# Two levels of a gated unit's decay tree in one TensorE step, on copies made by ScalarE

## The chip, the cores and the metric

The kernel runs on one core of a Trainium2 chip. The metric is device time in microseconds (us) of one execution, as the median of several runs. TensorE (PE) does the matrix products, VectorE (DVE) and ScalarE (ACT) the elementwise work, GpSimd (POOL) clears tiles, SyncE (SP) issues nearly all transfers.

## The reference

One decoder layer over 2048 tokens of width 1024, in f32. Its first half mixes tokens with three kinds of heads in parallel; the second half is a gated MLP of width 2816 with a causal convolution of width 3. The change is in the first half, in the heads that compute

```
S_t = diag(exp(log_f_t)) S_{t-1} + k_t^T v_t,   o_t = q_t S_t
```

for HGRN2 heads (forget gate from a sigmoid) and GLA heads (low-rank gate). Here the decay differs for each key channel and token, so within a chunk the scores are

```
attn[i, j] = sum_d q[i, d] k[j, d] exp(cum[i, d] - cum[j, d]),   j <= i
```

which is no plain product of q and k. The third kind, retention, has one decay for a head and needs no such care. Each head's output is normalised, gated, and the heads together go through one output projection.

## The kernel before

**Blocks and units.** The mixer works through four blocks of 512 tokens (`NB`, `TB`). In each block seven units follow each other in `ORDER`: h0, g, h1, h2, h3, r0, r1. An h unit is two HGRN2 heads (`unit_h`), g is four GLA heads in two halves (`unit_g`), r is two retention heads (`unit_r`). A unit begins with its input projections: long rows of f32 products, each split in three passes (`split3`, lines 290 to 292) of a high and a low part. They are TensorE's main stream. What is left of a unit is small work in many dependent steps, which is laid between the products of later units. After the last unit of a block come the output projection (`out_half`, `out_finish`) and the next block's norm. After block 3 follows the MLP, in products that the change does not touch.

**A gated unit (`gated`).** Scores inside 128 tokens are built by a tree. `LEVELS` are 1, 2, 4, 8, 16, 32, 64. At level s, queries in the odd runs of s tokens meet keys in the even run just ahead. Between two levels, q of the odd runs and k of the even runs are multiplied in place by the decay of a run (`tree[li]`, lines 743 and 745, on DVE), so that at each level a plain product gives the right scores. A level step is thus: 16 to 32 small products in tiles of 32 columns into a bank `lev` (line 737), then on DVE the two multiplications in place, which must wait until TensorE has read the old values, and then the scores go to their places: by a masked copy into `near` (line 749, up to level 16) or by ACT into the score tile `at` (line 756). At level 16 ACT also copies `near` into `at` (line 760). Ahead of the levels, products "dots" (`dt`) give the diagonal, which line 722 lays into `near`. Behind the levels k is transposed (`kT`), then come the products u with the update of the state (`carry`), the outputs o (`attn_out`), their norm and gate (`post`), and, some time later, their transpose (`transposed`) for the output projection.

**The order.** TensorE's order is written out by hand, that of the other engines is partly planned by priorities (`tc.high_priority`). A planner's clock (`Clock`) counts the nominal time of the products emitted so far (`adv`). A step that must wait for other engines is not emitted at once; its generator yields a gap, and the next step is emitted into the stream when that time has passed. `chain` lets one gated unit or retention unit at a time go through its steps; at `yield None` the next may begin. A tuple as a gap is a ride (`ride`): from its first time on the step goes right behind the next level step (`clock.pick`), at its second time at the latest alone. `until` runs due steps ahead of their time if something must be done by then. The constants of the gaps stand in lines 50 to 55:

```
LEVEL_GAP = (3.2, 4.2)
POST_GAP = 14.0
LAND = 6.0
FIRST_GAP = 1.8, 0.8
RIDE = (1.8, 6.0), (3.4, 7.6)
STAT_GAP, NORM_GAP = 2.4, 1.6
```

`LEVEL_GAP` lies between levels (h units, g units), `FIRST_GAP` behind the dots and after level 1, `RIDE` ahead of u and o, `POST_GAP` ahead of the transpose of an output. `STAT_GAP` and `NORM_GAP` space the parts of the norms, `LAND` is the time that a sum of weights waits for its loads.

**Side work.** DVE also computes sums for the MLP's block products (`weight_sums`, `early_sums`) and products of the conditioning vector (`ada`). These are tied behind a DVE instruction that was noted last (`marked`, `pinned`), so that they aren't put ahead of it.

Of the kernel before, what the change touches and what calls it, by code (L numbers as in the profile page):

```python
# [122 lines left out]
def trunk(ctx, tc, xT, vecs, cvec, cst, rope, msk, wada, win, walow, wgla, wout, wup, wdown, out):  # L123
# [125 lines left out]
    def marked(op):  # L249

        mark[:] = [op.ins]
# [317 lines left out]
    def norm1_stat(b):  # L569
        acc = new_acc(f"n1_{b}")  # L570

        def part(k):
            x = tmp(f"x{b}_{k}")
            nc.sync.dma_start(x[:], xT[b, :, k, :])
            sumsq(acc, x, k, f"n1_{b}_")
        for k in range(KD):
            clock.at(STAT_GAP * k, lambda k=k: part(k))
        bc1[b] = new_bc1(b)
        clock.ride(rstd(acc, f"n1_{b}", bc1[b][:], lambda: done.add(("n1", b)), gap=14.0), 24.0, 28.0)

# [27 lines left out]
    def tok_evac(vsg, pss):  # L608
        v, sg = vsg
        for j, ps in enumerate(pss):  # L610
            p3 = ps[:].rearrange("p (c n) -> p c n", n=256)
            c2 = slice(2 * j, 2 * j + 2)
            S.copy(v[:, c2, :], p3[:, :, 0:P])
            S.activation(sg[:, c2, :], p3[:, :, P:256], AF.Sigmoid)
            V.tensor_tensor(sg[:, c2, :], sg[:, c2, :], p3[:, :, P:256], op=ALU.mult)

    def tok_evac4(vsg, pss, at):

        v, sg = vsg
        for c, ps in enumerate(pss):  # L620
            gate = ps[:, at + P:at + 256]
            S.copy(v[:, c, :], ps[:, at:at + P])
            S.activation(sg[:, c, :], gate, AF.Sigmoid)
            V.tensor_tensor(sg[:, c, :], sg[:, c, :], gate, op=ALU.mult)

    def post(o, sg, name):
# [9 lines left out]
        V.tensor_tensor(o8, o8, rs[:].unsqueeze(2).to_broadcast([P, 8, 64]), op=ALU.mult)  # L636
        V.tensor_tensor(o[:], o[:], sg[:], op=ALU.mult)

# [27 lines left out]
    def carry(b, Sst, ps, decay):  # L666

        W = wide.pop(0)
        wide.append(W)
        at = pu.tile([P, NCH - 1, 64], F32, tag="Sc", name="Sc", bufs=3)  # L670
        halves = slice(0, 64), slice(64, P)
# [28 lines left out]
    def gated(name, b, ui, pos, kq, q, decay, subs, qk, sel):  # L700
# [14 lines left out]
        nh = 2 * len(subs)  # L715
        ps = late_ps("dt" + name)
        for c in range(NCH):
            tiled(ps[:, c * nh:(c + 1) * nh], qk[:, c * P:(c + 1) * P], sel)
        pairs = ps[:, 0:NCH * nh].rearrange("p (a n) -> p a n", n=len(subs))
        with tc.high_priority(offset=CHAIN):  # L720
            for i, near in enumerate(nears):
                V.copy_predicated(near[:], m_all[:, 80:112].unsqueeze(1).to_broadcast([P, 8, 32]),
                                  pairs[:, :, i:i + 1].to_broadcast([P, 8, 32]))
        adv(ML)
        yield FIRST_GAP[0]
        for li, s in enumerate(LEVELS):
            w = max(32, 2 * s)
            cols = slice(0, 128 if s < 64 else 256)
            pss = [lev_ps(f"lv{name}_{s}") for _ in parts]
            for c in range(NCH):  # L730
                for k0 in [g for g in range(0, P, 32) if g % w < max(s, 32)]:
# [3 lines left out]
                    for ps, rs in zip(pss, parts):  # L735
                        rhs = q[rs, :, at:at + w].rearrange("p h (n t s) -> p h n t s", t=2, s=s)[:, :, :, 1, :]
                        T.matmul(ps[p0:p0 + 32, n * w:(n + 1) * w].rearrange("p (h n s) -> p h n s", h=2, s=s),
                                 kq[rs, c * P + k0:c * P + k0 + 32], rhs, start=True, stop=True)
            with tc.high_priority(offset=CHAIN):
                ev = tree[li]  # L740
                nn = TB // (2 * s)
                qv = q[:].rearrange("p h (n t s) -> p h n t s", t=2, s=s)[:, :, :, 1, :]
                V.tensor_tensor(qv, qv, ev[:, :, 0:1].unsqueeze(1).to_broadcast([P, 2, nn, s]), op=ALU.mult)
                kv = kq[:].rearrange("p (n t s) -> p n t s", t=2, s=s)[:, :, 0, :]
                marked(V.tensor_tensor(kv, kv, ev[:, :, 1:2].to_broadcast([P, nn, s]), op=ALU.mult))
                for ps, at, near in zip(pss, attns, nears):
                    if s <= 16:
                        mk = m_all[:, 16 * li:16 * li + 16].rearrange("p (n s) -> p n s", s=s)
                        V.copy_predicated(near[:].rearrange("p a (n t s) -> p a n t s", t=2, s=s)[:, :, :, 1, :],
                                          mk.unsqueeze(1).to_broadcast([P, 8, 16 // s, s]),  # L750
                                          ps[:, cols].rearrange("p (a n s) -> p a n s", a=8, s=s))
                    else:
                        for r0 in range(0, P, w):
                            for odd in range(2):
                                p0 = r0 + s * odd
                                S.copy(at[r0:r0 + s, :].rearrange("p (c o h n) -> p c o h n", c=2, o=2, h=2)[:, :, odd, :, r0 + s:r0 + w],
                                       ps[p0:p0 + s, cols].rearrange("p (c h n) -> p c h n", c=2, h=2))
                    if s == 16:
                        for r0 in range(0, P, 32):
                            S.copy(at[r0:r0 + 32, :].rearrange("p (a n) -> p a n", a=8)[:, :, r0:r0 + 32],  # L760
                                   near[r0:r0 + 32])
            adv(ML)
            clock.pick()
            if s < LEVELS[-1]:
                yield LEVEL_GAP[two] + (FIRST_GAP[1] if s == 1 else 0.0)
        yield None
        yield LEVEL_GAP[two]
        ps = late_ps("kT" + name)
# [38 lines left out]
    def unit_h(b, u, pos):  # L807
# [38 lines left out]
    def unit_g(b, pos):  # L846
# [32 lines left out]
        for i in range(2):  # L879
# [3 lines left out]
            subs.append((rows, *tok_tiles(f"{nm}_{i}")))  # L883
        clock.chain(gated(nm, b, 4, pos, kq, q, decay, subs, qk, selg), 14.0)
        pss = tf512(f"vg{nm}", 18)
# [5 lines left out]
    def unit_r(b, r, pos):  # L891
# [16 lines left out]
        for x, y in zip(a, bb):  # L908
# [136 lines left out]
    def out_half(b, half, acc=None, after_pieces=None, begun=(), own=None):  # L1045
        all_done()
        for i in range(4):
# [3 lines left out]
            for m in (2 * i, 2 * i + 1):  # L1051
# [696 lines left out]
```

## Time and profile before

| what | value |
|---|---|
| median of 3 runs | 2422.54 us (2421.09 to 2425.87) |
| the profiled execution's own time | 2418.1 us |
| its span, first to last instruction | 2416.3 us |
| busy of TensorE | 2382.3 us, 99% |
| busy of VectorE | 1811.7 us, 75% |
| busy of ScalarE | 1229.3 us, 51% |
| busy of GpSimd | 154.2 us, 6% |
| mean granted TensorE clock | 0.998 |

The span is shorter than the execution's own time by what lies around the instructions. Busy time is the union of an engine's instructions; TensorE's overlap in its pipeline, so that the mean length of one is longer than the distance from one start to the next. In the groups of instructions, a row gives line, engine, operation, output and inputs by the program's names, shapes and count, then busy time, mean ns of one, and the engine's idle time just ahead of them with what ended it.

### The profile page before, as it was taken

The numbers are of one execution on the slowest core, as the hardware profiler recorded it, in microseconds if no ns is written. First come the engines' busy times: TensorE is split into PE (matmuls) and PEld (weight loads), VectorE is DVE, ScalarE is ACT, GpSimd is POOL, SyncE is SP. The second block draws the span as 40 slices with busy tenths as digits, with TensorE's granted clock in tenths as the row PEclk, the third lists the DMA queues.
The fourth block names the chain that finished last, engine by engine and source line by source line (L and its number), as shares of the span: only waits on it lengthen the run. The fifth ranks groups of instructions, "written<-read, shape, count | busy, mean of one in ns | idle before, by whom it ended". The sixth has DMA issues, their size and how long they took to land.

```text
span 2416.3 us, 51796 instructions
## 1 busy us (share of the span) xinstructions
PE 2382.3 (99%) x20523; PEld 1962.8 (81%) x20523; DVE 1811.7 (75%) x3391; ACT 1229.3 (51%) x2191; POOL 154.2 (6%) x275
## 2 busy tenths in 40 slices
PE   7999999999999999999999999999999999999998
PEld 5788878878788878888788888888878888888887
DVE  7687766877577746767988888966878787778666
ACT  4565445644565446535645554554545454555442
POOL 1000000000000000001000000000010110000000
PEclk9999999999999999999999999999999999999999
DMA  7665676896788758778554444686765444447663
GB/s 273 228 214 186 226 271 224 293 329 237 258 311 290 259 187 284 267 260 295 178 170 155 148 155 144 229 281 218 226 204 173 144 149 139 153 151 271 210 196 118
DMA packets 228883, 525.78 MB, mean 218 GB/s; under 512 B 25848, under 2 KB 28832, under 8 KB 228640
## 3 DMA queue, kind: packets, MB, share of 16 engines
q1 hardware_dynamic: 225440, 511.98, 63.1%
q0 software_dynamic: 3200, 10.49, 1.2%
q8 instruction: 161, 2.64, 0.4%
q14 instruction: 82, 0.67, 0.1%
HBM read 392.87 MB, written 129.50 MB: 216 GB/s over the span
## 4 chain that ended last, share of the span: by engine, by line
PE 84%; DVE 6%; DMA 5%; issue 3%; ACT 1%; SPq 0%; POOL 0%; DVEq 0%; ACTq 0%; POOLq 0%
PE X L290 6%; PE X L291 6%; PE X L292 6%; PE Z L291 3%; PE Z L292 3%; PE Z L290 3%; PE dX L290 3%; PE dX L292 3%; PE dX L291 3%; PE psqkvgr L290 3%; PE psqkvgr L291 2%; PE psqkvgr L292 2%; PE psvgh L290 2%; PE y L290 2%; PE y L291 2%
## 5 line engine op out<-in xcount | busy, mean ns | idle before, releaser
L290 PE MATMUL X<-B,A 128*128 128x512 f32 x572 | 223.1, 390 | 0.5 <-ACT u L1424 0.3
L291 PE MATMUL X<-B,A 128*128 128x512 f32 x572 | 222.8, 389 | 0.3 <-DVE B L1121 0.2
L292 PE MATMUL X<-B,A 128*128 128x512 f32 x572 | 222.6, 389 | 0.0
L1121 DVE TENSOR_TENSOR dA<-rd,dA 128x512 fp32r<-128x512 f32 x154 | 106.1, 690 | 89.8 <-ACT dA L1120 89.6
L1120 ACT CAST dA<-rd 128x512 fp32r<-128x512 f32 x154 | 95.6, 621 | 143.7 <-PE dX L292 58.0
L290 PE MATMUL dX<-dB,dA 128*128 128x512 f32 x396 | 154.1, 389 | 1.3 <-DVE y L1606 1.3
L292 PE MATMUL dX<-dB,dA 128*128 128x512 f32 x396 | 154.0, 389 | 0.0
L291 PE MATMUL dX<-dB,dA 128*128 128x512 f32 x396 | 154.0, 389 | 0.0
L1121 DVE TENSOR_TENSOR A<-s,A 128x512 fp32r<-128x512 f32 x176 | 120.6, 686 | 39.5 <-ACT A L1120 39.4
L290 PE MATMUL psvgh<-hvgh,ha 128*128 128x256 f32 x480 | 140.3, 292 | 0.0
L1120 ACT CAST A<-s 128x512 fp32r<-128x512 f32 x176 | 108.5, 617 | 56.9 <-PE Z L292 41.9
L291 PE MATMUL psvgh<-lvgh,ha 128*128 128x256 f32 x480 | 135.6, 283 | 0.0
L292 PE MATMUL psvgh<-hvgh,ha 128*128 128x256 f32 x480 | 135.6, 282 | 0.0
L290 PEld LDWEIGHTS X<-B,A 128*128 128x128 f32 x572 | 107.3, 188 | 24.0 <-ACT u L1424 1.1
L291 PEld LDWEIGHTS X<-B,A 128*128 128x128 f32 x572 | 107.4, 188 | 23.0 <-DVE B L1121 1.0
L292 PEld LDWEIGHTS X<-B,A 128*128 128x128 f32 x572 | 107.4, 188 | 22.3
L291 PE MATMUL Z<-B,A 128*128 128x512 f32 x308 | 120.5, 391 | 1.4 <-DVE B L1121 1.2
L290 PE MATMUL Z<-B,A 128*128 128x512 f32 x308 | 120.3, 391 | 0.1
L292 PE MATMUL Z<-B,A 128*128 128x512 f32 x308 | 119.9, 389 | 0.0
L1120 ACT CAST A<-r 128x512 fp32r<-128x512 f32 x132 | 82.3, 623 | 63.8 <-PE Z L292 58.5
L1121 DVE TENSOR_TENSOR A<-r,A 128x512 fp32r<-128x512 f32 x132 | 90.6, 687 | 31.8 <-ACT A L1120 31.6
L1121 DVE TENSOR_TENSOR dB<-rb,dB 128x512 fp32r<-128x512 f32 x154 | 105.6, 687 | 9.9 <-ACT dB L1120 9.5
(480 smaller groups left out, 6714.3 us busy)
## 6 DMA issues: line engine op xcount, KB each, us to landing
gs<-yv SPq DMA_DIRECT2D x154, 256.0 KB, 3.0
rb<-gs SPq DMA_DIRECT2D x154, 256.0 KB, 4.2
r<-wup SPq DMA_DIRECT2D x143, 256.0 KB, 3.5
s<-sumsu SPq DMA_DIRECT2D x132, 256.0 KB, 3.0
wada<-wada SPq DMA_DIRECT2D x48, 512.0 KB, 4.9
rd<-sumsd SPq DMA_DIRECT2D x88, 256.0 KB, 3.9
rd<-wdown SPq DMA_DIRECT2D x66, 256.0 KB, 3.8
x<-xT SPq DMA_DIRECT2D x64, 256.0 KB, 5.9
```

What stands on the lines that cost most here:

```text
L290: T.matmul(ps, lhs[0], rhs[0], start=first, stop=False, skip_group_check=more)
L291: T.matmul(ps, lhs[0], rhs[1], start=False, stop=False, skip_group_check=more)
L292: T.matmul(ps, lhs[1], rhs[0], start=False, stop=last, skip_group_check=more)
L1120: S.copy(hi, src)
L1121: V.tensor_tensor(lo, src, hi, op=ALU.subtract)
```

## The change

- The levels go in pairs (1, 2), (4, 8), (16, 32); 64 stays alone. For a pair, ACT copies the odd runs of q and all of k to new tiles `qc` and `kc_` (`ahead`); then DVE scales q and k in place for the second level (`faded`). TensorE then does the first level from the copies and the second from q and k, in one step into one bank. After it DVE scales q and k for the next level, ACT copies again, both levels are laid into their places (`laid`), and DVE scales once more.
- The dots go into the first pair's step.
- The gaps: between pairs 5.2 us (h) and 6.4 us (g), 7.6 us ahead of the first pair, 4.0 us ahead of `kT`; `yield None` comes behind the pair (16, 32) instead of behind level 64. Chains start 1.5 us earlier after their call.
- Outputs are transposed 21 us after their step, rides of state updates get later windows, loads and norms get more time; a sum of squares is emitted 3 us after its load.
- More DVE instructions are `marked`: gates, the end of `post`, and the residual sums of the output projection.
- The tile `Sc` has 2 buffers instead of 3.
- Retention units of block 2 start after 14.5 instead of 11 us.

```diff
-POST_GAP = 14.0
-LAND = 6.0
-FIRST_GAP = 1.8, 0.8
-RIDE = (1.8, 6.0), (3.4, 7.6)
-STAT_GAP, NORM_GAP = 2.4, 1.6
+POST_GAP = 21.0
+LAND = 7.5
+FIRST_GAP = 7.6
+PAIR_GAP = (5.2, 6.4)
+RIDE = (2.4, 7.4), (3.8, 9.0)
+STAT_GAP, STAT_LAND, NORM_GAP = 2.4, 3.0, 2.0
...
-            sumsq(acc, x, k, f"n1_{b}_")
+            clock.at(STAT_LAND, lambda: sumsq(acc, x, k, f"n1_{b}_"))
...
-        clock.ride(rstd(...), 24.0, 28.0)
+        clock.ride(rstd(...), 26.0, 30.0)
...
+    qc = p1.tile([P, 2, TB // 2], F32, tag="qc", name="qc")
+    kc_ = p1.tile([P, TB], F32, tag="kc", name="kc")
...
-            V.tensor_tensor(sg[:, c2, :], sg[:, c2, :], p3[:, :, P:256], op=ALU.mult)
+            marked(V.tensor_tensor(sg[:, c2, :], sg[:, c2, :], p3[:, :, P:256], op=ALU.mult))
...
+        def faded(li):
+            s, ev = LEVELS[li], tree[li]
+            nn = TB // (2 * s)
+            qv = q[:].rearrange("p h (n t s) -> p h n t s", t=2, s=s)[:, :, :, 1, :]
+            V.tensor_tensor(qv, qv, ev[:, :, 0:1].unsqueeze(1).to_broadcast([P, 2, nn, s]), op=ALU.mult)
+            kv = kq[:].rearrange("p (n t s) -> p n t s", t=2, s=s)[:, :, 0, :]
+            marked(V.tensor_tensor(kv, kv, ev[:, :, 1:2].to_broadcast([P, nn, s]), op=ALU.mult))
+        def ahead(li):
+            s = LEVELS[li]
+            S.copy(qc[:].rearrange("p h (n s) -> p h n s", s=s),
+                   q[:].rearrange("p h (n t s) -> p h n t s", t=2, s=s)[:, :, :, 1, :])
+            S.copy(kc_[:], kq[:])
+        def level(li, first):
...
+                        T.matmul(ps[p0:p0 + 32, o + n * w:o + (n + 1) * w].rearrange("p (h n s) -> p h n s", h=2, s=s),
+                                 (kc_ if first else kq)[rs, c * P + k0:c * P + k0 + 32], rhs, start=True, stop=True)
+        def laid(li, first):
...
+        with tc.high_priority(offset=CHAIN):
+            ahead(0)
+            faded(0)
+        yield FIRST_GAP
+        for li in range(0, 8, 2):
+            pss = [lev_ps(f"lv{name}_{li}") for _ in parts]
+            pair_ = li < 6
+            if li == 0:
+                dots = late_ps("dt" + name)
+                for c in range(NCH):
+                    tiled(dots[:, c * nh:(c + 1) * nh], qk[:, c * P:(c + 1) * P], sel)
+            if pair_:
+                level(li, True)
+                level(li + 1, False)
+            else:
+                level(li, False)
+            with tc.high_priority(offset=CHAIN):
+                faded(li + 1 if pair_ else li)
+                if li < 4:
+                    ahead(li + 2)
+                if li == 0:
+...
+                laid(li, pair_)
+                if pair_:
+                    laid(li + 1, False)
+                if li < 4:
+                    faded(li + 2)
+            adv((2 if pair_ else 1) * ML)
+            clock.pick()
+            if li == 4:
+                yield None
+            if pair_:
+                yield PAIR_GAP[two]
+        yield 4.0
...
-        clock.chain(gated(nm, b, u, pos, kq, q, decay, subs, qk, selh), 9.0 if b == u == 0 else 6.0)
+        clock.chain(gated(nm, b, u, pos, kq, q, decay, subs, qk, selh), 7.5 if b == u == 0 else 4.5)
...
-        clock.chain(retention(nm, b, r, pos, a[0], kk, kc, q, vsg), 14.5 if b < 2 else 11.0)
+        clock.chain(retention(nm, b, r, pos, a[0], kk, kc, q, vsg), 14.5 if b < 3 else 11.0)
...
-                    V.scalar_tensor_tensor(x1[m], ps[:], G1[:, m:m + 1], x1[m], op0=ALU.mult, op1=ALU.add)
+                    marked(V.scalar_tensor_tensor(x1[m], ps[:], G1[:, m:m + 1], x1[m], op0=ALU.mult, op1=ALU.add))
```

More of the change, by code (lines that the diff above doesn't have):

```diff
@@ L578, in norm1_stat @@
         bc1[b] = new_bc1(b)
-        clock.ride(rstd(acc, f"n1_{b}", bc1[b][:], lambda: done.add(("n1", b)), gap=14.0), 24.0, 28.0)
+        clock.ride(rstd(acc, f"n1_{b}", bc1[b][:], lambda: done.add(("n1", b)), gap=14.0), 26.0, 30.0)
     def norm1_h(b):
@@ L715, in gated @@
         nh = 2 * len(subs)
[L716 to L726, printed above, removed]
+        def faded(li):
[11 more added lines that the diff above has]
+        def level(li, first):
+            s = LEVELS[li]
             w = max(32, 2 * s)
-            cols = slice(0, 128 if s < 64 else 256)
-            pss = [lev_ps(f"lv{name}_{s}") for _ in parts]
+            o = 0 if first else 128
             for c in range(NCH):
@@ new lines, in laid @@
+        def laid(li, first):
+            s = LEVELS[li]
+            w = max(32, 2 * s)
+            o = 0 if first else 128
+            cols = slice(o, o + (128 if s < 64 else 256))
+            for ps, at, near in zip(pss, attns, nears):
+                if s <= 16:
+                    mk = m_all[:, 16 * li:16 * li + 16].rearrange("p (n s) -> p n s", s=s)
+                    V.copy_predicated(near[:].rearrange("p a (n t s) -> p a n t s", t=2, s=s)[:, :, :, 1, :],
+                                      mk.unsqueeze(1).to_broadcast([P, 8, 16 // s, s]),
+                                      ps[:, cols].rearrange("p (a n s) -> p a n s", a=8, s=s))
+                else:
+                    for r0 in range(0, P, w):
+                        for odd in range(2):
+                            p0 = r0 + s * odd
+                            S.copy(at[r0:r0 + s, :].rearrange("p (c o h n) -> p c o h n", c=2, o=2, h=2)[:, :, odd, :, r0 + s:r0 + w],
+                                   ps[p0:p0 + s, cols].rearrange("p (c h n) -> p c h n", c=2, h=2))
+                if s == 16:
+                    for r0 in range(0, P, 32):
+                        S.copy(at[r0:r0 + 32, :].rearrange("p (a n) -> p a n", a=8)[:, :, r0:r0 + 32],
+                               near[r0:r0 + 32])
@@ new lines, in gated @@
+        with tc.high_priority(offset=CHAIN):
[12 more added lines that the diff above has]
+                level(li + 1, False)
+            else:
+                level(li, False)
+            with tc.high_priority(offset=CHAIN):
+                faded(li + 1 if pair_ else li)
+                if li < 4:
+                    ahead(li + 2)
+                if li == 0:
+                    pairs = dots[:, 0:NCH * nh].rearrange("p (a n) -> p a n", n=len(subs))
+                    for i, near in enumerate(nears):
+                        V.copy_predicated(near[:], m_all[:, 80:112].unsqueeze(1).to_broadcast([P, 8, 32]),
+                                          pairs[:, :, i:i + 1].to_broadcast([P, 8, 32]))
+                laid(li, pair_)
[4 more added lines that the diff above has]
+            adv((2 if pair_ else 1) * ML)
+            clock.pick()
+            if li == 4:
+                yield None
+            if pair_:
+                yield PAIR_GAP[two]
```

41 lines of the change are left out of this document (7 added, 34 removed).

## The prediction

> **What bounds the kernel now.** I read the page first, then busy time by stage, then TensorE's own waits, then single steps in the timeline.
>
> ```profile
> span 2416.3 us, 51796 instructions
> ...
> PE 2382.3 (99%) x20523; PEld 1962.8 (81%) x20523; DVE 1811.7 (75%) x3391; ACT 1229.3 (51%) x2191; POOL 154.2 (6%) x275
> ```
>
> TensorE is busy in 99% of the span; nothing else is near. So the time falls only if TensorE gets less to do or waits less. The mixer, where the change lies, runs from about 60 to 1110 us. The next view is busy time by stretch (columns: stretch, length, busy of PE, PEld, DVE, ACT, POOL, then clock and DMA; the last row sums four stretches).
>
> ```profile
> 330.00:620.00 290.00, 286.84 (x3817) 233.88 (x3816) 206.93 (x521) 145.64 (x300) 13.61 (x24) 1.00 0.77 266
> ...
> sum 1050.00, PE 1043.46 PEld 859.14 DVE 748.33 ACT 545.60 POOL 52.24; mean PE 260.87 PEld 214.78 DVE 187.08 ACT 136.40 POOL 13.06
> ```
>
> The granted clock is 1.00 here, and TensorE idles 1050.00 - 1043.46 = 6.5 us. That is all that better timing of steps could give. Its longest wait there, in the list of waits:
>
> ```profile
> PE lvh L737 <- DVE orsh L180: 1.5, 1, 1.5
> ```
>
> If there is more to win it is hidden in "busy": what a small block costs TensorE when it cuts into the stream of large products. One level step of an h unit, with its neighbours (columns: start, length, engine, line, what):
>
> ```profile
> 308.80 0.39 PE L291 MATMUL y<-oTh,hwo 128*128 128x512 f32 x1
> 309.03 0.39 PE L292 MATMUL y<-oTh,lwo 128*128 128x512 f32 x1
> 309.35 0.46 PE L737 MATMUL lvh<-qbh,kh 128*32 128x32 f32 x32
> 309.74 0.51 PE L290 MATMUL y<-oTr,hwo 128*128 128x512 f32 x1
> 310.08 0.40 PE L291 MATMUL y<-oTr,hwo 128*128 128x512 f32 x1
> ...
> 313.36 0.46 PE L737 MATMUL lvh<-qbh,kh 128*32 128x32 f32 x32
> ```
>
> Large products follow each other every 0.23 us (308.80 to 309.03). From 309.03 to 310.08 there are 1.05 us for two of them, 0.46 us, and the step: the step takes 0.59 us. Of this 0.09 lies ahead of the level (309.35 against 309.26), and 0.11 in the first large product behind it, which lasts 0.34 to the next start. The same for a unit g, whose step has twice as many:
>
> ```profile
> 114.71 0.28 PE L291 MATMUL psvgh<-lvgh,ha 128*128 128x256 f32 x1
> 114.83 0.28 PE L292 MATMUL psvgh<-hvgh,ha 128*128 128x256 f32 x1
> 115.04 0.76 PE L737 MATMUL lvg<-qbg,kg 64*32 64x32 f32 x64
> 115.72 0.39 PE L290 MATMUL psvgh<-hvgh,ha 128*128 128x256 f32 x1
> 115.95 0.28 PE L291 MATMUL psvgh<-lvgh,ha 128*128 128x256 f32 x1
> ```
>
> 115.95 - 114.83 = 1.12, less two smaller products of 0.12 (114.71 to 114.83), is 0.88 us for 64 against 0.59 for 32. So 32 matmuls cost about 0.29 us, and merely going in and out costs 0.59 - 0.29 = 0.30 us, whatever is done inside.
>
> **The change, part by part.**
>
> *Two levels to a step.* Each of 20 units (16 h, 4 g) has seven level steps; with pairs (1,2), (4,8), (16,32) and 64 alone there are four. Three passages fewer, 60 in all: 60 x 0.30 = 18.0 us less on TensorE. The matmuls are the same in number and shape. The first of a pair reads copies that lie without strides, and I take no difference for that. The bound on the passage is between 0.20 (the two edges alone) and 0.30, so 12 to 18; the g row, measured whole, speaks for 18. The Trainium skill, "TensorEngine Tiling (Array Packing)", section Key Properties, says that a change of tiling mode drains TensorE; that is the passage. Its section Instruction Overhead gives a matmul some 60 cycles at least, which by the clock in the same skill's "Trainium Kernel Development and Optimization" is an estimated 0.20 us for 32 matmuls over four tiles, so a passage of 0.39 and a sum of 23 us; the trace's 0.29 for 32 is the measured one and I keep it.
>
> *The dots go into the first pair.* A block of dots behind a level, and one alone:
>
> ```profile
> 163.38 0.39 PE L292 MATMUL pshfh<-ha,lhfh 128*128 128x512 f32 x1
> 163.69 0.64 PE L737 MATMUL lvh<-qbh,kh 128*32 128x128 f32 x16
> 164.16 0.45 PE L149 MATMUL dth<-c_all,qkh 128*32 128x2 f32 x32
> 164.54 0.50 PE L290 MATMUL pshfh<-ha,hhfh 128*128 128x512 f32 x1
> 164.88 0.40 PE L291 MATMUL pshfh<-ha,hhfh 128*128 128x512 f32 x1
> ...
> 574.82 0.28 PE L292 MATMUL psvgh<-hvgh,ha 128*128 128x256 f32 x1
> 575.02 0.43 PE L149 MATMUL dth<-c_all,qkh 128*32 128x2 f32 x32
> 575.39 0.38 PE L290 MATMUL psvgh<-hvgh,ha 128*128 128x256 f32 x1
> 575.61 0.28 PE L291 MATMUL psvgh<-lvgh,ha 128*128 128x256 f32 x1
> ```
>
> Alone they take 0.79 - 0.24 = 0.55 us. Behind a level the whole step takes 1.50 - 0.46 = 1.04; with a level step of 0.59 that leaves 0.45. So company saves a block of dots 0.10 us, not 0.30, and some ride already. I take 0.04 for each of 20: 0.8 us, bounds 0 and 6 (20 x 0.30).
>
> *Fewer steps to ride on.* The state updates (products u and o, 44 in all with two o for each g) ride behind a level step if one falls in their window. Before, the first window is 4.2 us long and level steps of the same unit kind come every 3.2 + 0.5 = 3.7 us of the planner's clock, so one always falls in. After, the window is 5.0 or 5.2 and steps come every 5.2 + 1.0 = 6.2. So one in six goes alone: 44 x 0.17 = 7.5, at 0.30 us each a loss of 2.3 us; bounds 0 and 13 (all alone).
>
> *The longer hand-over.* This is where the change adds a wait. Before, the next level needs two DVE products. After, the next pair needs: q and k scaled for the second level (DVE), both copied (ACT), the near blocks laid (DVE), q and k scaled once more (DVE). Groups of instructions of the mixer (busy us, mean ns, then idle before):
>
> ```profile
> L743 DVE TENSOR_TENSOR qbh<-qbh,eh 128x512 f32<-128x512 f32 x96 | 65.9, 687 | 35.4 <-PE lvh L737 35.2
> ...
> L745 DVE TENSOR_TENSOR kh<-kh,eh 128x256 f32<-128x256 f32 x96 | 40.2, 419 | 0.0
> ...
> L749 DVE COPY_PREDICATED nearh<-m_all,lvh 128x128 f32<-128x128 uint32 x80 | 28.1, 351 | 0.0
> ```
>
> ```profile
> L760 ACT COPY ath<-nearh 32x256 f32<-32x256 f32 x64 | 25.8, 403 | 10.7 <-DVE nearh L749 5.5 <-DVE nw L183 3.3 <-DVE nw L184 1.4
> ...
> L828 ACT COPY qbh<-sqh 64x512 f32<-64x512 f32 x30 | 18.6, 620 | 35.2 <-DVE sqh L826 35.0
> ...
> L756 ACT COPY ath<-lvh 32x128 f32<-32x128 f32 x64 | 16.4, 256 | 1.0 <-PE lvh L737 0.3
> ```
>
> With idle engines DVE needs 0.69 + 0.42 + 2 x 0.35 + 0.69 + 0.42 = 2.92 us. The copies (128x512 each, nearest row 0.62) lie beside this: 0.69 + 0.62 + 0.62 + 0.42 = 2.35. Before it is 0.69 + 0.42 = 1.11. The room: a nominal gap of 3.2 us gave 313.36 - 309.81 = 3.55 above, so 5.2 gives some 5.5. Slack before 3.55 - 1.11 = 2.4, after 5.5 - 2.9 = 2.6: as much, but three engines' queues have to be free in place of one. How late DVE can be, around a step of an h unit:
>
> ```profile
> 183.71 0.46 PE L737 MATMUL lvh<-qbh,kh 128*32 128x32 f32 x32
> 184.90 0.63 ACT L388 ACTIVATE sqn<-x 128x512 f32<-128x512 f32 x1 [1.30 <-DMA x<-xT]
> 185.57 0.69 DVE L389 TENSOR_TENSOR san<-san,sqn 128x512 f32<-128x512 f32 x1 [2.29 <-ACT sqn L388]
> 186.18 0.68 DVE L632 TENSOR_REDUCE omsh<-osqh 128x8 f32<-128x512 f32 x1
> 186.77 0.68 DVE L743 TENSOR_TENSOR qbh<-qbh,eh 128x512 f32<-128x512 f32 x1
> 187.44 0.42 DVE L745 TENSOR_TENSOR kh<-kh,eh 128x256 f32<-128x256 f32 x1
> 188.01 0.43 PE L737 MATMUL lvh<-qbh,kh 128*32 128x32 f32 x29
> ```
>
> The level ended at 184.17, DVE came 2.6 us later, because it stood behind a sum of squares that waited for ACT and a DMA; k was ready at 187.86, 0.15 us before its reader. And the list of waits for DVE and ACT in the mixer:
>
> ```profile
> DVE qbh L743 <- PE lvh L737: 43.1, 28, 3.8
> ```
>
> ```profile
> ACT hhfh L278 <- PE pshqh L291: 17.5, 8, 3.6
> ```
>
> DVE stood ready at 28 steps of 112 of the h units, so it is behind other work at the rest. ACT stands up to 3.6 us before a weight cast whose buffer TensorE has not freed, and a copy queued behind that comes late. With the lateness shown (2.6) a full hand-over takes 5.5 us and just fits; with one such ACT wait more it does not. There are 40 full hand-overs (1,2 to 4,8 and 4,8 to 16,32 in 20 units); I take a stall of 0.75 us at one in ten: 3 us, bounds 0 and 32 (0.8 at each). The step from 16,32 to 64 needs no copy.
>
> *Level 64 of units g* needs the two banks of 16,32 back: eight copies of 0.40 and eight of 0.26 on ACT, 5.3 us, behind 1.1 + 0.35 on DVE, against a gap of 6.4 + 0.35. This just fails to have slack; 4 x 0.25 = 1 us, bounds 0 and 8 (ACT 2 us late each).
>
> *ACT's copies* add 6 x 20 x 0.62 = 74 us to 546 in 1050, 59%. Cover: ACT's idle time; without it casts of weights come late, which is the same wait as above.
>
> *Sums of squares 3 us behind their DMA, sums and products of the conditioning tied behind newer work.* They take from DVE's queue waits such as the 2.29 above. Direct gain at most the 6.5 us of idle; I take 1 us. Their instructions, DMAs on SP's queue among them, stay the same.
>
> *Outputs transposed 21 instead of 14 us on, norms and landing later, one bank less for the carried states, first step of a pair chain at 4.5 + 7.6 = 12.1 us after its call instead of 6.0 + 0.5 + 2.6 = 9.1.* Taken at nothing. The chain of one unit occupies the line 7.6 + 3 x 1.0 + 2 x 5.2 = 21.0 us where it was 25.8 (0.5 + 1.8 + 0.8 + 7 x 0.5 + 6 x 3.2), so the later start doesn't push the next unit. At a block's end the planner pulls a due transpose forward when it runs out of products, so it comes no later than now; should post-work not be done then, this costs up to 2 us in each of four blocks.
>
> *The sum* against the profiled execution (span 2416.3, own time 2418.1): -18.0 - 0.8 + 2.3 + 3.0 + 1.0 - 1.0 = -13.5 us, 2404.6. The median of the runs shown, 2422.54, lies 4.4 above that execution; on its scale the forecast is 2409.0.
>
> **The rivals.**
>
> *The hand-over over ACT becomes the bound (slower).* If the 2.6 us of slack is regularly used up by DVE's lateness, each wait on ACT stalls TensorE in full. For it: 84 of 112 steps find DVE busy, and two casts of 1.05 us stand in ACT's queue for each piece of weights. Against: DVE idles 29% of the mixer and both kinds of work are issued ahead of others. Half a cast (0.53) at each of 40 hand-overs is 21 us: -13.5 - 3 (in the sum already) + 21 = +4.7 to +7.5 with the g units' copies late too, 2427 to 2430. It decides from (13.5 + 4.8 + 3) / 40 = 0.53 us for each hand-over on. The Trainium skill ("Trainium Kernel Development and Optimization", Best Practices) speaks for this one: it warns that tiling speeds up TensorE but not the emptying of PSUM. Chance 0.20.
>
> *The passages come back (no change).* Riders, dots and transposes that go alone: if half of 44 riders do, 22 x 0.30 = 6.6, with passages worth 0.20 (12 us): -12 + 6.6 + 3 = -2.4, 2420. Against it: the windows are widened along with the gap. Chance 0.12.
>
> *More is saved.* Passage 18, dots 3, no lone riders, half of the idle gone: -24, 2398. This needs ACT never late. Chance 0.08.
>
> **How the numbers follow.** Forecast as summed 0.60, its own range 2401 to 2416. The measurement can tell about 0.2%, 4.8 us. Faster by over that: 0.60 + 0.08 = 0.68; within it 0.12; slower 0.20. The range goes from 2398 to 2430, the nearer ends of the outer cases, which leaves out 0.05 below and some 0.10 above.
>
> **What would show it.** Right: level blocks of 64 with about 0.88 us a step in h units; TensorE's busy time down by 14 to 18 us; waits of level and of state products on DVE or ACT below 10 us in the mixer; ACT up by 70 us. Wrong: TensorE's waits for q, k or their copies of over 20 us; more than ten u or o blocks alone; a pair step well above 0.9 us, so that the matmuls themselves and not the passage were the price.

## The result: 0.3% slower, and the profile after

The changed kernel takes 2430.3 us (median of 21 runs, 2424.94 to 2438.99), the kernel before 2422.7 (21 runs, 2419.87 to 2430.53). The ratio is 1.0031, interval [1.0022, 1.0040]: slower by some 7.6 us where 13.5 less was forecast. The profiled execution of the changed kernel took 2435.79, one of its longer ones. Its page begins:

```profile
span 2433.8 us, 51912 instructions
...
PE 2372.3 (97%) x20523; PEld 1967.2 (81%) x20523; DVE 1815.2 (75%) x3391; ACT 1293.1 (53%) x2311; POOL 154.6 (6%) x275
```

TensorE is busy 10.0 us less (2372.3 against 2382.3), and yet the span is 17.5 us longer: busy has gone from 99% to 97%. ACT has its 120 copies. The difference lies in the mixer. This is busy time by stretch, from the first input projection to the last transposed output, for the kernel before and then for the changed one (columns as in the prediction):

```profile
57.70:1115.80 1058.10, 1051.57 (x14452) 865.84 (x14451) 749.57 (x1874) 547.31 (x1125) 52.24 (x93) 1.00 0.74 257
```

```profile
57.60:1129.20 1071.60, 1042.00 (x14451) 870.30 (x14451) 753.64 (x1874) 612.16 (x1244) 51.64 (x92) 0.99 0.73 254
```

The stretch is 13.5 us longer with 9.6 us less busy time, so TensorE idles 29.6 us where it idled 6.5. The granted clock reads 0.99. Those are the two things to look at; first the saving itself. A pair step between the same large products as in the prediction (timeline of the changed kernel, TensorE):

```profile
597.78 0.39 PE L292 MATMUL y<-oTh,hwo 128*128 128x512 f32 x1
598.01 0.39 PE L293 MATMUL y<-oTh,lwo 128*128 128x512 f32 x1
598.33 0.46 PE L751 MATMUL lvh<-qc,kc 128*32 128x32 f32 x32
598.60 0.49 PE L751 MATMUL lvh<-qbh,kh 128*32 128x32 f32 x32
599.02 0.50 PE L291 MATMUL y<-oTh,hwo 128*128 128x512 f32 x1
599.35 0.39 PE L292 MATMUL y<-oTh,hwo 128*128 128x512 f32 x1
```

From 598.01 to 599.35 there are 1.34 us for two large products (0.46) and the pair: 0.88 us, where two single steps took 2 x 0.59 = 1.18. The passage of 0.30 is gone, as worked out. Now TensorE's waits in the mixer (us in total, times, longest):

```profile
PE kTh L816 <- DVE kh L727: 7.0, 4, 2.5
PE oh L150 <- issue: 4.9, 3, 1.8
PE ssn L150 <- DVE san L390: 3.3, 2, 1.8
PE lvh L751 <- ACT kc L734: 2.3, 2, 1.5
PE lvh L751 <- ACT qc L732: 2.0, 1, 2.0
PE kTh L816 <- issue: 1.8, 1, 1.8
PE pshfh L291 <- DVE sgg L627: 1.3, 1, 1.3
PE ssn L150 <- DVE nearh L800: 1.2, 2, 1.0
PE lvh L751 <- DVE kh L727: 1.2, 3, 0.5
...
PE lvh L751 <- DVE qbh L725: 0.8, 2, 0.4
```

No single wait is large. The transposes of k lead (`kTh`), then products that stopped with no releaser in sight ("issue"), the sums of squares (`ssn`), and the pairs' hand-over (the four `lvh` rows here hold 6.3 us at 8 steps). And five times the clock was halved (the same view of busy time, on those stretches; the clock is the third number from the end):

```profile
340.80:344.20 3.40, 3.40 (x10) 2.58 (x8) 1.21 (x8) 0.00 (x0) 0.00 (x0) 0.50 0.95 342
477.30:484.10 6.80, 6.52 (x74) 5.10 (x64) 6.32 (x22) 2.21 (x5) 0.00 (x0) 0.50 0.85 302
624.10:627.50 3.40, 3.40 (x10) 2.62 (x9) 1.30 (x8) 0.00 (x0) 0.00 (x0) 0.50 0.06 24
723.10:726.50 3.40, 2.93 (x14) 2.96 (x15) 3.30 (x8) 1.78 (x6) 0.00 (x0) 0.50 0.98 327
999.60:1003.00 3.40, 3.40 (x14) 3.01 (x13) 3.03 (x8) 2.68 (x6) 0.00 (x0) 0.50 0.79 266
```

That is 20.4 us at half speed, which costs half of it, 10.2 us. It counts as busy, which is why the busy time shows only 9.6 of the saving: 9.6 + 10.2 = 19.8 us of TensorE's work are gone. So 13.5 us more = -19.8 saved + 23.1 idle + 10.2 half clock; the rest of the profiled difference (17.7 by own times) is idle behind the mixer, 10.3 against 5.8.

One profile could be a chance. The mean granted clock is recorded for every run: 0.9946 over the 21 runs of the changed kernel, 0.9979 over the 69 runs of the kernel before beside the experiments. 0.0033 of 2430 us is 8.0 us more lost to the half clock in the mean, as large as the whole loss of 7.6.

How a stop and the half clock hang together is seen at one of these transposes (timeline of the changed kernel, in order of time; the first row is level 64 of this unit):

```profile
715.31 0.64 PE L751 MATMUL lvh<-qbh,kh 128*32 128x128 f32 x16
...
718.83 0.69 DVE L725 TENSOR_TENSOR qbh<-qbh,fh 128x512 f32<-128x512 f32 x1
...
721.80 0.68 DVE L725 TENSOR_TENSOR qbh<-qbh,eh 128x512 f32<-128x512 f32 x1
722.41 0.68 DVE L639 TENSOR_TENSOR og<-og,orsg 128x512 f32<-128x512 f32 x1
723.01 0.42 DVE L727 TENSOR_TENSOR kh<-kh,eh 128x256 f32<-128x256 f32 x1
...
723.57 1.08 PE L816 MATMUL kTh<-c_all,kh 128*128 128x128 f32 x4 [2.53 <-DVE kh L727]
...
724.67 0.41 PE L292 MATMUL psvgh<-lvgh,ha 128*128 128x256 f32 x1
724.88 0.41 PE L293 MATMUL psvgh<-hvgh,ha 128*128 128x256 f32 x1
```

k must be scaled once more after level 64 (line 727, at 723.01) before it is transposed. The level ended at 715.95. DVE first did sums of weights, the first scaling of q of the next unit (718.83, by `fh`), which the earlier `yield None` had let in, and the norm of g's output (722.41 is a part of it); q of the unit itself came at 721.80 (ACT's copy in line 822, a step of this unit, waits for it), k last. TensorE stopped for 2.53 us, and the products after it start every 0.21 us (724.67 to 724.88) where 0.12 was seen at full clock. Some 2.9 us of the stretch of half clock lie behind the stop, and half of that, 1.5 us, comes on top of the 2.53.

### The profile page after: what moved, and what is told of

It reads as the page before. It is cut to its first block, busy times and chain, and to the rows that moved or that the text cites. A ratio compares the mean times of both kernels' runs of the same rounds, so it can differ in the third digit from the quotient of the medians.

```text
span 2433.8 us, 51912 instructions
## 1 busy us (share of the span) xinstructions
PE 2372.3 (97%) x20523; PEld 1967.2 (81%) x20523; DVE 1815.2 (75%) x3391; ACT 1293.1 (53%) x2311; POOL 154.6 (6%) x275
## 3 DMA queue, kind: packets, MB, share of 16 engines
q8 instruction: 161, 2.64, 0.4%
## 4 chain that ended last, share of the span: by engine, by line
PE 74%; DVE 11%; DMA 7%; ACT 4%; issue 2%; SPq 0%; DVEq 0%; POOL 0%; ACTq 0%
PE X L291 6%; PE X L293 6%; PE X L292 6%; PE Z L292 3%; PE Z L293 3%; PE Z L291 3%; PE dX L292 3%; PE dX L293 3%; PE dX L291 3%; PE psqkvgr L291 3%; PE psqkvgr L292 2%; PE psqkvgr L293 2%; DMA wada<-wada 2%; PE Y L291 2%; PE Y L293 2%
```

## The experiments

The expectations name theories by letters. A: the pairs save what was forecast, and stops at several places take it back. B: the hand-over over ACT is too short. C: the retimings cost. D: a stop of TensorE brings on the half clock. E: the half clock comes by itself. F: stops with no releaser are waits for the next instructions, after dense blocks of small products; G: they have nothing to do with density. H: the added ties make the waits of `ssn`. K: k of level 64 stands behind the next unit's work on DVE. L: a wait that is removed is followed by one at the next weak place.

For each profiled execution the mixer's length is split up, all from its trace: idle time of TensorE, of it the stops with no releaser ("issue"), half the length of the stretches at clock 0.50, and the rest. The ratio is to the kernel before on the same chip. The numbers are us.

| kernel | ratio, interval | mixer | idle | of it issue | half clock | rest |
|---|---|---|---|---|---|---|
| before | | 1058.0 | 6.5 | 1.4 | 0 | 1051.5 |
| after | 1.0031 [1.0022, 1.0040] | 1071.5 | 29.6 | 6.6 | 10.2 | 1031.7 |
| e1_kt7 | 1.0014 [1.0004, 1.0024] | 1058.8 | 22.6 | 5.7 | 1.7 | 1034.5 |
| e2_retime_only | 1.0015 [1.0004, 1.0025] | 1066.9 | 10.5 | 3.7 | 1.7 | 1054.7 |
| e3_pairs_only | 1.0072 [1.0058, 1.0087] | 1073.8 | 31.1 | 13.4 | 8.5 | 1034.2 |
| e4_stat30 | 1.0041 [1.0027, 1.0056] | 1066.1 | 28.5 | 6.6 | 3.4 | 1034.2 |
| e5_fill | 1.0128 [1.0113, 1.0143] | 1095.2 | 35.8 | 19.9 | 13.6 | 1045.7 |
| e6_apart | 1.0044 [1.0028, 1.0061] | 1065.7 | 21.2 | 11.6 | 3.4 | 1041.1 |
| e7_gap66 | 1.0156 [1.0143, 1.0170] | 1094.7 | 48.2 | 16.2 | 17.1 | 1029.5 |
| e8_both | 1.0072 [1.0060, 1.0084] | 1076.4 | 35.4 | 9.9 | 10.2 | 1030.7 |
| e9_early_kt | 1.0176 [1.0157, 1.0195] | 1107.3 | 37.2 | 4.2 | 18.8 | 1051.3 |
| e10_no_ties | 1.0033 [1.0021, 1.0046] | 1069.2 | 26.4 | 8.6 | 11.9 | 1030.9 |
| e11_next_later | 1.0058 [1.0044, 1.0071] | 1076.3 | 33.5 | 12.4 | 6.8 | 1035.9 |
| e12_kt7_no_ties | 0.9991 [0.9983, 1.0000] | 1056.1 | 19.1 | 5.4 | 3.4 | 1033.6 |
| e13_gap56 | 1.0014 [1.0006, 1.0023] | 1060.5 | 22.1 | 4.0 | 6.8 | 1031.5 |
| e14_kt6 | 1.0034 [1.0022, 1.0045] | 1069.8 | 28.2 | 8.5 | 10.2 | 1031.5 |

The last column is the change's saving: every kernel with pairs has 1029 to 1036 (but for e5, which adds products, and e6, which sets riders apart), the two without have 1051 to 1055. What the pairs save is there each time; idle time and half clock decide. (Where TensorE idles inside a stretch of half clock, the column counts some of it twice: 0.4 us in the changed kernel, at most 2.9, in e7 and e9.)

**One part at a time.** The transposes of k later:

```
-        yield 4.0        # ahead of kT
+        yield 7.0
```

> The change with the transpose of k 7.0 instead of 4.0 us behind level 64; nothing else. Theory A (pairs save some 20 us of TensorE, and waits at other steps together with half-clock stretches that follow them eat it): the four waits of kT for k (7.0 us in the changed kernel's profile) and one or two of the half-clock stretches (3.6 us each) go, 2418 to 2424, about 6 to 12 us under the changed kernel. Theory B (the hand-over over ScalarE between pairs is the bound): nothing of note, 2428 to 2433. Theory C (the later outputs, rides, landings and the ties of sums cost the time): 2426 to 2430.

The waits of `kTh` for `kh` are gone, one short stretch of half clock is left in place of five, and the time is 2425.39 against 2420.87 on that chip, a little above what A gave. So about half of the loss hung on this gap. The profile flatters it: over all 12 runs the mean granted clock is 0.9960 against 0.9946 for the changed kernel, 3.4 us less half clock and not 8.5. Two of the five stretches (723.1 and 999.6) had begun at these transposes.

The kernel before with the new gaps and ties, without pairs; the gaps of the levels stay as before:

```
-POST_GAP, LAND = 14.0, 6.0
-RIDE = (1.8, 6.0), (3.4, 7.6)
-STAT_GAP, NORM_GAP = 2.4, 1.6
+POST_GAP, LAND = 21.0, 7.5
+RIDE = (2.4, 7.4), (3.8, 9.0)
+STAT_GAP, STAT_LAND, NORM_GAP = 2.4, 3.0, 2.0
...
+        marked(V.tensor_tensor(o[:], o[:], sg[:], op=ALU.mult))
```

> The kernel before with everything of the change but the pairs: outputs at 21, rides, landings, norms, sums of squares 3 us behind their load, retention of block 2 later, more instructions noted for the ties; levels one to a step as before. Theory A: no more than 3 us from the kernel before, 2419 to 2426. Theory B: the same. Theory C: slower, 2428 to 2436.

2425.06 against 2420.87. The retimings alone cost some 4 us (1 to 6 by the interval), more than the 3 that A allowed and less than C gave.

The changed kernel with the same lines the other way round, pairs only:

```
-POST_GAP, LAND = 21.0, 7.5
+POST_GAP, LAND = 14.0, 6.0
...
-        marked(V.tensor_tensor(o[:], o[:], sg[:], op=ALU.mult))
+        V.tensor_tensor(o[:], o[:], sg[:], op=ALU.mult)
```

> The change's pairs with their gaps alone: outputs at 14, rides, landings, norms, sums of squares and ties as before the change. Theory A: near the changed kernel, 2424 to 2434, with the kT waits still there. Theory B: 2430 or more. Theory C: the pairs' gain shows, 2402 to 2414.

2438.79, 17.9 above before. The retimings help the pairs by some 10 us, so they are not what went wrong by themselves (C falls as the cause). Without them other waits lead (TensorE in the mixer, pairs only), and of the waits of `kTh` for `kh`, which A expected here as well, 0.8 us are left, although the next unit is let in as early and the gap ahead of kT is 4.0:

```profile
PE oh L150 <- issue: 9.8, 5, 2.9
PE lvg L751 <- ACT atg L770: 6.7, 6, 2.4
PE oTh L646 <- DVE oh L640: 3.5, 1, 3.5
PE uh L150 <- ACT kTh L819: 2.8, 2, 1.4
```

The norm's sums ride later, to take away the wait of `ssn`:

```
-        clock.ride(rstd(acc, f"n1_{b}", ...), 26.0, 30.0)
+        clock.ride(rstd(acc, f"n1_{b}", ...), 30.0, 34.0)
```

> The change with the first step of the norm's sum 30 to 34 instead of 26 to 30 us behind the first load. Theory A: the waits of ssn for the sum of squares (3.3 us in two, and 1.2 more) and up to two half-clock stretches of 3.6 us go, 2420 to 2428. Theory B: 2428 to 2433. Theory C: 2427 to 2432.

2430.41 against 2420.87, no better than the changed kernel: `ssn` still waits once for 2.4 us, the transposes of k wait as before (6.8 us, 4 times).

**Is it the hand-over?** A longer gap between pairs; k's transposes stay at 4.0:

```
-PAIR_GAP = (5.2, 6.4)
+PAIR_GAP = (6.6, 7.8)
```

> The change with 6.6 and 7.8 us between pairs instead of 5.2 and 6.4. Theory B (the hand-over of a pair over ScalarE is what costs most): 2415 to 2423. Theory A (it is one of several places): the waits of level products for q, k and their copies (6.3 us in the changed kernel) fall under 2, half a stretch of half clock less, 2422 to 2428; the waits of kT stay.

2459.29, the second slowest of all and far above what A and B gave. The waits of pairs for q, k and their copies are gone, those of k's transposes for k too (0.2 us), though their gap is as it was; others stand in their place:

```profile
PE ssn L150 <- DVE san L390: 8.8, 2, 7.5
PE lvh L751 <- issue: 7.7, 3, 3.3
PE lvg L751 <- DVE nearh L763: 7.6, 1, 7.6
```

The steps of a unit end later and run into the norm, the sums and the next unit. A longer hand-over doesn't help, so B falls, and L gains. A milder form with the rides and the norm moved along:

```
-PAIR_GAP = (5.2, 6.4)
-RIDE = (2.4, 7.4), (3.8, 9.0)
+PAIR_GAP = (6.0, 7.2)
+RIDE = (2.4, 8.4), (5.0, 11.0)
...
+        clock.ride(rstd(acc, f"n1_{b}", ...), 30.0, 34.0)
...
+        yield 7.0        # ahead of kT
```

> As e1_kt7, with 6.0 and 7.2 us between pairs, the norm's first step at 30 to 34 and rides at 2.4 to 8.4 and 5.0 to 11.0. Theory A: waits of kT, of the hand-over and half of those of ssn gone, idle of the mixer under 16 us: 2414 to 2421. Theory B: 2414 to 2421 as well, by the gap. Theory C: 2425 to 2430.

2439.5 against 2420.81 where A and B gave 2414 to 2421, with waits of `oh` for the state on ACT (4.9 us), of projections for a gate on DVE (4.1) and of `lvg` for the score tiles (3.5) in the lead. The riders set 0.9 us apart from the pair and from each other, with k's transposes at 7.0:

```
-            go()
+            self.at(0.9 * (n + 1), go)
```

> As e1_kt7, but a rider is emitted 0.9 us of large products behind the pair (the second rider 1.8 us) and no longer right behind it. Theory F (TensorE's stops of 0.4 to 1.8 us for nothing that the profile shows are waits for its next 16 KB of instructions, which a pair with a rider behind it uses up faster than they come): these stops fall from 5.7 us in e1_kt7 to under 2.5; against that some 35 passages more at 0.30 us, so the time without idle and half clock rises by 8 to 11 us, and the whole is 2427 to 2433. Theory G (they have nothing to do with density): the stops stay at 5 to 7 us, the time is 2431 to 2436.

2431.11. The rest grows by 7 us, as steps go alone again. The stops without releaser rose, to 11.6 us, where less dense blocks were to have fewer of them: a miss, to which the section on the hardware returns.

**Is it the stop that halves the clock?** Idle products (33, which the trace shows as 66 instructions every 0.22 us, 14 us in all; they go into a bank that the transposes then overwrite) ahead of some transposes of k, to fill the wait:

```
+        if b and ui == 2:
+            keep_going(ps, 11)
```

> The change with 11 idle products (128x256, some 2.5 us together) put on TensorE just ahead of the transpose of k of unit h2 in blocks 1 to 3, where the changed kernel waits 1.6 to 2.5 us for k. They only fill the wait. Theory D (an idle TensorE is what brings the half-clock stretches): the waits at these three places are gone from the list, no half-clock stretch starts there (two of five did in the changed kernel), and the time is the changed kernel's or some 1 to 4 us less, 2425 to 2430. Theory E (the stretches come by themselves, at any place): stretches still start there, and the time is the changed kernel's or a little more, 2429 to 2433.

2452.52 against 2420.81. The products went ahead of another unit's transposes than those that wait, so these still waited (4.4 us, 3 times) and the question wasn't answered. Stops without releaser came to 19.9 us. The cleaner test makes the wait in the kernel before, which has no half clock in its mixer:

```
-        yield LEVEL_GAP[two]   # ahead of kT, before
+        yield 0.6
```

> The kernel before the change with the transpose of k 0.6 instead of 3.2 or 4.2 us behind level 64; nothing else, no pairs. It makes TensorE wait for k on purpose: k is ready some 1.1 to 3.4 us behind a level there. Theory D (a stop of TensorE brings half-clock stretches): 10 to 20 waits of kT, 8 to 20 us, and one to four half-clock stretches of 3.4 us in the mixer, where the kernel before had none; 2428 to 2444. Theory E (the stretches come by themselves, or from the pairs): the waits without stretches, 2426 to 2436.

2464.49 against 2422.93. Its waits, and two of its seven stretches at half clock:

```profile
PE kTh L770 <- DVE kh L745: 16.0, 12, 3.1
PE ssn L149 <- DVE san L389: 5.6, 2, 5.3
```

```profile
446.50:453.30 6.80, 5.83 (x48) 4.68 (x49) 4.11 (x10) 5.02 (x10) 0.00 (x0) 0.50 0.96 336
736.60:743.40 6.80, 5.50 (x47) 4.45 (x48) 4.03 (x9) 4.12 (x8) 0.00 (x0) 0.50 0.42 147
```

The mixer grew by 49.3 us: 30.7 idle and 18.8 half clock, with the rest the same to 0.2 (to some 3 us without the double count). Four of the seven stretches begin at a stop of these transposes, the others at other stops that came along. So the half clock comes with stops of TensorE, without any pair: D is shown. The time is far above the 2444 that D allowed, since waits of other steps grew as well.

**Order on DVE.** The four `marked` taken out of the changed kernel, so that sums and conditioning products aren't tied behind new work:

```
-        marked(V.tensor_tensor(o[:], o[:], sg[:], op=ALU.mult))
+        V.tensor_tensor(o[:], o[:], sg[:], op=ALU.mult)
...
```

> The change without its four added marks: sums and products of the conditioning are tied as before the change, the gaps stay the change's. Theory A with the ties harmless: 2427 to 2433, as the changed kernel. Theory H (with the marks, DVE stands before a product of the conditioning whose load has not landed, 27.4 us in the changed kernel against 17.0 before, and this makes the waits of ssn): 2420 to 2427, DVE's waits for those loads near 17 us and ssn's waits for sums under 1.5 us.

2430.07 against 2422.93, the ratio of the changed kernel. DVE's wait in front of the conditioning products falls, from the first row (changed kernel) to the second (no ties), and the waits of `ssn` fall from 4.5 us to 0.3, as H has it; but those of k's transposes and the stops without releaser grow (third fence, TensorE without ties), and the time that H gave (2420 to 2427) is missed.

```profile
DVE wada L223 <- DMA wada<-wada: 27.4, 12, 4.3
```

```profile
DVE wada L223 <- DMA wada<-wada: 19.4, 10, 3.7
```

```profile
PE kTh L816 <- DVE kh L727: 8.1, 5, 2.5
PE oh L150 <- issue: 7.2, 3, 2.8
```

The next unit let in after level 64, as it was before:

```
-            if li == 4:
+            if li == 6:
                 yield None
```

> The change with the next unit let into the line behind level 64, as before the change, and not behind the pair (16, 32). Theory K (kT waits because the next unit's first scaling of q and k stands on DVE ahead of the scaling of k behind level 64): the waits of kT, 8.8 us, go to under 2, as in e1_kt7, with half-clock stretches behind them; 2420 to 2426. If sums of weights and the norm of g's output alone hold k back: the waits stay over 5 us, 2427 to 2433.

2435.97 against 2422.93, with TensorE's waits:

```profile
PE oh L150 <- issue: 8.9, 5, 2.2
PE uh L150 <- DVE nearh L800: 3.1, 1, 3.1
...
PE kTh L816 <- DVE kh L727: 1.5, 2, 0.8
```

K holds as to that wait (7.0 to 1.5 us), though not as its only condition, since e3 and e7 let the next unit in as early and have 0.8 and 0.2 us of it: what else stands on DVE at that time counts too. L holds as to the time: what was won there comes back elsewhere.

**Both together.** k's transposes at 7.0 and no ties:

```
-        yield 4.0        # ahead of kT
+        yield 7.0
...
-        marked(V.tensor_tensor(o[:], o[:], sg[:], op=ALU.mult))
+        V.tensor_tensor(o[:], o[:], sg[:], op=ALU.mult)
...
```

> The two edits that took a wait away, together: the transpose of k 7.0 us behind level 64 (e1_kt7) and the four marks taken back (e10_no_ties). Theory A (the pairs' gain is there and only waits, stops for instructions and half clock hide it): waits of kT and ssn both under 1.5 us, idle of the mixer 12 to 18 us, 2416 to 2423. Theory L (each wait taken away only moves the same time to the next weak place): idle stays at 20 us or more, 2424 to 2431.

2419.11 against 2420.48, level with before, and 0.9991 / 1.0031 = 0.9960 of the changed kernel. Its mixer and longest waits:

```profile
57.80:1114.00 1056.20, 1037.13 (x14452) 868.28 (x14451) 751.48 (x1874) 611.58 (x1244) 51.63 (x92) 1.00 0.74 257
```

```profile
PE ssn L150 <- DVE san L390: 3.6, 2, 2.3
PE lvh L751 <- DVE kh L727: 2.0, 3, 1.1
PE lvh L751 <- issue: 2.0, 2, 1.6
PE oTg L646 <- DVE oTg L651: 1.8, 2, 1.5
```

17.9 us saved in the rest, 12.6 given back in idle time, 3.4 in half clock. The time is the one that A gave; the idle time, 19.1 us, lies between A's (12 to 18) and L's (20 or more). `ssn` waits 3.6 us without the ties, where it waited 3.1 with them at the same gap (e1), so H doesn't hold here. Two small steps from it, a longer gap between pairs and a shorter one ahead of kT:

```
-PAIR_GAP = (5.2, 6.4)
+PAIR_GAP = (5.7, 6.9)
```

> As e12_kt7_no_ties, with 5.7 and 6.9 us between pairs. Theory A: waits for q, k and their copies under 1.5 us, 2414 to 2421. Theory L: 2424 to 2434, as in e7_gap66, where longer gaps made other waits.

```
-        yield 7.0        # ahead of kT
+        yield 5.8
```

> As e12_kt7_no_ties, with 5.8 instead of 7.0 us ahead of the transpose of k. Theory A: 2416 to 2424, kT's waits under 3 us. Theory L: 2424 to 2431.

2424.09 and 2429.91 against 2420.48, both as L gave them. With the longer pair gap `ssn` waits 6.6 us; with the shorter kT gap `uh` waits 8.2 us for DVE. Neither way leads on; no version was found that is clearly faster than the kernel before.

## Why the prediction was wrong

**The saving was right.** Passages, dots and lone riders came to 18.0 + 0.8 - 2.3 = 16.5 us; the rest fell by 19.8, and by 15.6 to 22 in the other kernels with pairs that leave the riders as they are and add nothing. Counted in the two timelines, 230 blocks of small products cut into the large ones before, 162 after: 68 x 0.30 = 20.4. The 60 forecast passages are among these. The count doesn't give the spread between the kernels with pairs: e12 has some 18 blocks fewer than the changed kernel and saves 17.9, which stays open. Lone riders were mis-sized: 10 u or o blocks stand alone where 8 did, not 7.5 more, so 0.6 us and not 2.3.

**Level 64 of units g** cost nothing (1.0 was taken): its block has no wait.

**The longer hand-over**, put at 3.0, took 6.3 us at 8 steps. Right in kind, half the size, and short of the 20 us at which the text would have named it the bound.

**The step that failed** is that the sum has waits at the pairs and nowhere else. The transposes of k, 4.0 us behind level 64, have no term; the earlier `yield None` entered only as a line that is free sooner (21.0 against 25.8 us), not as work of the next unit in front of k on DVE. In the changed kernel the transposes waited 7.0 us for k. Outputs, norms and landings were "taken at nothing" and the ties and later sums of squares as a gain of 1.0; these retimings alone cost some 4 us (e2). `ssn` waits 4.5 us in the changed kernel, and sums of squares stand behind conditioning products that wait for a DMA (27.4 us on DVE; 17.0 before). The ties lengthen that wait on DVE also without pairs (24.1 in e2), but `ssn` waits nowhere in e2 and does in e12 without the ties, so that they alone make its waits is not shown. In all, TensorE's idle time grew by 23.1 us, where the sum had 3.0 + 1.0 for the hand-over and level 64, less 1.0. The text asked what is late next only for the pairs; other steps had moved against each other as well.

**Two terms were missing.** The half clock (10.2 us in the profile, 8.0 by the clock of all runs), and the stops without releaser (from 1.4 to 6.6 us, a part of the idle time). The kernel before had no half clock in its mixer and one such stop of 1.0 us, so their price couldn't be read off; but a kernel that idles 6.5 us in 1050 has little experience of stops, and each new one was priced at its bare length.

**The rival that gave 2427 to 2430** hit the number with another mechanism: ACT's hand-over. ACT's copies cost 64.8 us of its time (74 was taken) and are waited for 4.3 us in the rows above, and with a longer gap for the hand-over (e7) the time rose. That the number came out was luck.

**The signs** that were to show the forecast right came out for the most part: 0.88 us for a pair step, ACT up by some 65 us, and under 10 us of waits of level and state products on DVE or ACT. They looked at the pairs alone, and so could not show the loss. Only busy time, down by 10.0 instead of 14 to 18 us, pointed at it, because time at half clock counts as busy.

Still open is how the waits fall. From e12 to e13 and e14 one gap moves by 0.5 or 1.2 us and the time by 5 or 11 us. The mean granted clock of all their runs goes from 0.9970 to 0.9947 and 0.9946, worth 5.6 and 5.8 us, so half clock can be most of the first step and half of the second. The waits are single profiles of plans in which everything behind the moved step is shifted, and no run tells which shift did it.

## What to carry to other kernels

In a kernel with its critical engine busy 99%, price a change by what it does to the order at each step that it moves, and not only at the step that it is meant for: 20 us saved on the engine were given back by waits at half a dozen steps, of 1 to 7 us in all each, and the half clock behind them. Count a stop of TensorE of 2 us or more at more than its length: the stretch of half clock that tended to follow here cost up to 1.7 us, or 3.4 where it was a long one. A merge of small steps should come with the gaps behind it tuned again; here that moved the result from +0.3% to level, and no further.

## What the runs showed of the hardware

**Short stops halve TensorE's clock.** In the 16 traces 64 stretches of 3.41 or 6.83 us at clock 0.50 lie between 60 and 2380 us (two expectations put one at 3.6), and each has a stop of TensorE of 0.98 us or more that ends within 4.5 us of its start. Longer stops do it more often (a stretch with two such stops near it counts at both):

| stop, us | stops | with half clock |
|---|---|---|
| 0.7 to 1.0 | 50 | 2 |
| 1.0 to 1.4 | 56 | 3 |
| 1.4 to 1.7 | 47 | 9 |
| 1.7 to 2.1 | 32 | 12 |
| 2.1 to 2.5 | 23 | 17 |
| over 2.5 | 31 | 24 |

The Trainium skill ("TensorE: Matmul & The Clock Gate", Part 1: The HAM clock gate) has the clock halved after a whole idle window of some 3.4 us, with windows that run freely. The lengths of the stretches agree with such a window; the stops that were enough here were for the most part shorter, many of them 1.4 to 2.5 us.

**TensorE stops at the bounds of its code.** The instructions come in packets of 16 KB (page of the changed kernel: packets, MB, share):

```profile
q8 instruction: 161, 2.64, 0.4%
```

2.64 MB in 161 packets are 16.4 KB each. One stop without releaser, in the midst of a block of small products that lacks nothing else (changed kernel):

```profile
114.79 0.40 PE L150 MATMUL oh<-W,qbh 128*32 128x128 f32 x8
115.01 0.22 PE L150 MATMUL oh<-vh,ath 128*32 128x64 f32 x1
117.04 0.37 PE L150 MATMUL oh<-vh,ath 128*32 128x64 f32 x12 [1.81 <-issue]
```

Counted over TensorE's instructions, nearly all such stops above 0.7 us fall at number 193 or 194 of 256 (1473 and 2241 in the changed kernel: 5 x 256 and 8 x 256, plus 193), which is where one packet would end and the next begin; each ends 2.2 to 2.9 us after a packet of that queue began. They come only where the code before runs fast: of 1818 such bounds in the mixers of 16 traces, 77 of the 578 whose last 128 instructions took under 2.5 us have a stop over 0.35 us, 11 of the 607 with 2.5 to 6 us, none of the 633 above. Small products are such code, and a pair step holds twice as many in a row: 44 bounds have such fast code (under 2.5 us) ahead of them in the changed kernel, 26 in the kernel before. Where a bound falls changes with every instruction put in or moved ahead of it, which fits e5 and e6, where such stops grew with little else; that was not tried by itself. The Trainium skill ("Runtime: NRT & Kernel Launch", Instruction fetch mechanics) has blocks of this size and 256 instructions, and calls their crossing mostly hidden; the runs agree for slow code and not for such dense blocks.
